# The recurrent block's gate of a decoder layer, multiplied in float32r parts

## The chip, the cores and the metric

The kernel runs on one core of a Trainium2 chip. The metric is the device time of one execution in microseconds (us), the median of several runs. TensorE is called PE in the profile (its weight loads PEld), VectorE DVE, ScalarE ACT, GpSimd POOL and SyncE SP.

## The reference

One decoder layer on 256 tokens with 2048 features in float32: a SwiGLU block, a mixer, cross attention into a memory, a second SwiGLU block and a last norm. The mixer is a sliding window attention beside an RWKV-7 time mixing. This is the part of the time mixing that the change touches:

```python
r, k, v, xw, xa, xg = jnp.split(xs, c, axis=-1)      # xg: 160 features
g = jax.nn.sigmoid(xg) @ g2.astype(f32)              # g2: (160, 1024)
...
y = rwkv7_scan(r, decay, k, v, -kk, kk * a)
mean = jnp.mean(y, axis=-1, keepdims=True)
var = jnp.mean(jnp.square(y - mean), axis=-1, keepdims=True)
y = ((y - mean) * lax.rsqrt(var + GN_EPS)).reshape(B, T, RWKV_WIDTH)
y = y * ln_w.astype(f32) + ln_b.astype(f32)
bonus = jnp.sum(r * k * r_k, axis=-1, keepdims=True) * v
y = (y + bonus.reshape(B, T, RWKV_WIDTH)) * g
```

The gate g is a product of 256 tokens x 160 features with 160 x 1024 weights. The result y is then multiplied by w_proj_rwkv.

## The kernel before

**Products in parts.** The large products don't run in float32. Each operand is split into two float32r parts: the high part is a cast on ACT (L345 for weights, L668 for activations), the low part is the rest, a subtraction on DVE (L346, L669). A product is then the sum of three float32r products, high x high, high x low and low x high (`times`, L438 to L440), accumulated in PSUM. Weights come in items of two blocks of 128 features by 512 columns; an item is used by 12 products (two blocks, two halves of the tokens, three parts). There are three buffers each for the high and the low parts (`hi`, `lo`), so the parts of an item are made up to two items ahead, and a cast can start when the item three before it has been used. A smaller float32 product, as those of the recurrent chain, takes its operands directly.

**Order of the work.** The large products run one after the other (`product`). After every six of TensorE's products there is a tick, at which each of several groups of background generators (`bg`: attn, ew, inverse, chain, norm and others) takes one step up to its next `yield`. Instructions are created in that order; a scheduler then orders each engine's queue by readiness, so that an engine's order can differ from the code's.

**The recurrent block.** It has two halves (h=0, 1) of 512 features each. `shifted` makes its inputs from the products with w_in (names r0, v0, r1, v1 are marked as seen when one is done); it uses a tile with the tag "d". `values(h)` turns v, `chain(h)` runs the recurrence and marks y0 or y1, and `finish(h)`, in the group norm, which runs one generator at a time, does the rest:

- it loads the half's columns of g2 (L1545, L1546) into a tile of two 128-row blocks, the last 32 of the 160 features in rows 96 to 127 of the second block, whose first 96 rows are set to zero (L1544);
- it takes the pair of tiles "sq" in `parted`, high and low (one buffer each, which `removal_keys` and `values` use too; the mark "parts" lets one user in at a time, `alone`), squares y into them (L1552, L1553, L1555), and sums the squares by head on TensorE (`head_sums`, L1154 with bdmean); ACT takes the root (L1557), DVE the reciprocal in four pieces with two ticks between (L1561) and the product with y (L1563);
- it multiplies the gate, float32, on TensorE (L1568): for each of four column blocks c of 128, two products of 128 rows with 256 token columns, the sigmoid of xg as the moving operand (`xg`, two blocks laid out as g2: the last 32 features in rows 96 to 127 of the second);
- DVE applies ln_w, the bonus, ln_b and the gate (L1574, L1577), and the result is split into `yr` (L668, L669), which the product with w_proj_rwkv reads.

While this runs, the foreground multiplies the four column blocks of the second gate by w_in (`gr`, L1598), and then uses yr.

Of the kernel before, what the change touches and what calls it, by code (L numbers as in the profile page):

```python
# [8 lines left out]
F32R = mybir.dt.float32r  # L9
AF = mybir.ActivationFunctionType  # L10
ALU = mybir.AluOpType
# [4 lines left out]
P = 128  # L16
T = 256
# [125 lines left out]
def decoder_layer(ctx: ExitStack, tc: tile.TileContext, a: dict, out: bass.AP):  # L143
    nc = tc.nc
    act, dve, pool, pe = nc.scalar, nc.vector, nc.gpsimd, nc.tensor
# [7 lines left out]
    bg = Interleave()  # L153
# [9 lines left out]
    def f32(x):  # L163
        return x.bitcast(F32)
# [4 lines left out]
    def two():  # L169
        return ps.tile([P, 2, 512], F32, tag="two", name="two", bufs=2)  # L170
# [18 lines left out]
    def wait_for(name):  # L189
        while name not in bg.seen:  # L190
            yield

    def idle(n):
        for _ in range(n):
            yield
# [96 lines left out]
    raws, parts = {}, {}  # L292
# [157 lines left out]
    def combinations(sp, x, seven, early, ready, tag, apart):  # L450
# [43 lines left out]
        return c  # L494

    def product_pair(x: Act, c, w, four, seven, early, after, end, finish, first=()):


# [33 lines left out]
        for q in range(late + 1):  # L532
# [22 lines left out]
            for i in range(KU):  # L555
                for to, t, j in (("p2", 0, 0), ("p4", 1, 0), ("p3", 0, 1), (p5, 1, 1)):
                    off = to == "p3" and q in early
                    ends = last and i == KU - 1
                    add(to, of_c(q, i) if off else of_x(t, k + i), u[i][j], ends)
                    if ends:  # L560
                        finish(to, b)
                    if t:
                        bg.tick()
# [3 lines left out]
    def gate_up(sp, x, c, r, w):  # L567
        hb = sp.tile([P, 2, 512], F32, tag="hb", name="hb", bufs=2)
        u2, u3 = (sp.tile([P, 512], F32, tag="u", name="u", bufs=2) for _ in range(2))

        def after(b):
            act.copy(hb[:, 0], b["p1"])

        def end(b):
            dve.tensor_tensor(u2[:], b["p6"], hb[:, 0], ALU.add)
            dve.tensor_tensor(u3[:], b["p7"], u2[:], ALU.add)
            dve.tensor_tensor(u2[:], b["p5"], u2[:], ALU.add)
            while c["next"]:
                bg.spawn("feat", c["next"].pop())

        def finish(to, b):
            if to == "p2":
                dve.tensor_tensor(hb[:, 0], b["p2"], hb[:, 0], ALU.add)
                act.activation(hb[:, 0], hb[:, 0], AF.Silu, scale=r[0])
            elif to == "p4":
                dve.tensor_tensor(hb[:, 1], b["p4"], u3[:], ALU.add)
                act.activation(hb[:, 1], hb[:, 1], AF.Silu, scale=r[1])
            else:
                t, v = (0, u2) if to == "p3" else (1, u3)
                dve.tensor_tensor(v[:], b[to], v[:], ALU.add)  # L590
                dve.scalar_tensor_tensor(
                    hb[:, t], v[:], r[t], hb[:, t], ALU.mult, ALU.mult
                )

        product_pair(x, c, w, False, SEVEN, EARLY, after, end, finish)
        return hb
# [69 lines left out]
    def split(x: Act, c, n, src):  # L666

        act.copy(x.at(0, c, n), src)  # L668
        dve.tensor_tensor(x.at(1, c, n), src, f32(x.at(0, c, n)), ALU.subtract)  # L669
        x.done |= set(range(c, c + n))  # L670
# [171 lines left out]
    with tc.tile_pool(name="f1", bufs=1, reuse_waits="tile") as sp:  # L842
        aligned(sp)
        at["pool"] = sp
        x = sp.tile([P, 2, D], F32, name="x")
# [46 lines left out]
    with tc.tile_pool(name="mx", bufs=1, reuse_waits="tile") as sp:  # L892
        aligned(sp)

        def t4(name, shape=(P, 4, T), dt=F32):
            return sp.tile(list(shape), dt, tag="t4", name=name, bufs=N4)
# [180 lines left out]
        xwa, xg = xs[:, 0, :], xs[:, 1:, :]  # L1077
# [66 lines left out]
        def parted(name):  # L1144
            return [
                sp.tile([P, 2, 512], F32R, tag=name + e, name=name + e, bufs=1)
                for e in ("hi", "lo")
            ]

        def head_sums(bd, parts):  # L1150
            b = two()
            for i in range(2):
                for j, part in enumerate(parts):
                    pe.matmul(b[:, i], bd[:], part[:, i], start=j == 0, stop=j == 1)  # L1154
            return b

        def alone():
            while "parts" in bg.seen:
                yield
            bg.seen.add("parts")  # L1160

        def wide4(x):
            return x[:].rearrange("p (a c) t -> p a (c t)", a=2)
# [103 lines left out]
        for n in range(4):  # L1267
            pg = product(n2.x, W["w_in"])
            g = t4("ga", (P, 2, 512))
# [54 lines left out]
        def room(name, shape):  # L1324
            return sp.tile(list(shape), F32, tag="mk", name=name, bufs=NMK)
# [81 lines left out]
        ek = dict(skip_group_check=True)  # L1407
# [127 lines left out]

        yr = Act([], [], 4)

        def finish(h):
            yield from wait_for(f"y{h}")
            for part in yr.parts:  # L1540
                part.append(t4("yr", dt=F32R))
            g2 = room("g2", (P, 2, 4 * P))
            f4 = slice(4 * h * P, (4 * h + 4) * P)
            pool.memset(g2[:96, 1, :], 0.0)  # L1544
            pool.dma_start(g2[:, 0, :], W["rwkv_g2"][:P, f4])  # L1545
            pool.dma_start(g2[96:, 1, :], W["rwkv_g2"][P:, f4])  # L1546
            y = yq[h]
            sq = room("sq", (P, 4, T))
            v = wide4(sq)
            yield from alone()  # L1550
            parts = parted("sq")
            act.activation(parts[0][:], wide4(y), AF.Square)  # L1552
            act.activation(sq[:], y[:], AF.Square)  # L1553
            yield
            dve.tensor_tensor(parts[1][:], v, f32(parts[0][:]), ALU.subtract)  # L1555
            yield from idle(2)
            act.activation(v, head_sums(bdmean, parts)[:], AF.Sqrt, bias=gneps[:])  # L1557
            bg.seen.discard("parts")
            yield
            for i in range(4):  # L1560
                dve.reciprocal(sq[:, i], sq[:, i])  # L1561
                yield from idle(2)
            dve.tensor_tensor(y[:], y[:], sq[:], ALU.mult)  # L1563
            yield
            b = two()[:].rearrange("p a (c t) -> p (a c) t", c=2)
            for c in range(4):
                for m in range(2):
                    pe.matmul(  # L1568
                        b[:, c], g2[:, m, c * P : (c + 1) * P], xg[:, m, :],
                        start=c % 2 + m == 0, stop=m == 1, **ek,  # L1570
                    )
            for c in range(4):
                f = slice(4 * h + c, 4 * h + c + 1)
                dve.scalar_tensor_tensor(  # L1574
                    y[:, c], y[:, c], ln_w[:, f], bv[h][:, c, :], ALU.mult, ALU.add
                )
                dve.scalar_tensor_tensor(y[:, c], y[:, c], ln_b[:, f], b[:, c], ALU.add, ALU.mult)  # L1577
                if c % 2:
                    split(yr, 4 * h + c - 1, 2, y[:, c - 1 : c + 1])
                    yield  # L1580
# [13 lines left out]
        for n in range(4):  # L1594
            pg = product(n2.x, W["w_in"])
            g = t4("gr", (P, 2, 512))
# [15 lines left out]
        for n in range(4):  # L1612
            m = t4("ml", (P, 2, 512))
            if n in kept:
                g = kept[n]
            else:
                g = t4("gl", (P, 2, 512))
# [79 lines left out]
        for mb in range(2):  # L1697
            for h in range(4):
                pe.matmul(
                    b4[h // 2][:, h % 2], vm[:, mb, h * P : (h + 1) * P], pt[mb][:, h, :],  # L1700
                    start=mb == 0 and h % 2 == 0, stop=mb == 1, skip_group_check=True,
# [13 lines left out]
    with tc.tile_pool(name="f2", bufs=1, reuse_waits="tile") as sp:  # L1715
        aligned(sp)
        at["pool"] = sp
        x = sp.tile([P, 2, D], F32, name="x")
# [110 lines left out]
```

## Time and profile before

| what | us |
|---|---|
| median of 3 runs (lowest 2220.95, highest 2223.41) | 2220.98 |
| the profiled execution | 2222.56 |
| its span, from the first to the last instruction | 2220.8 |
| DVE busy | 1759.2 |
| ACT busy | 1193.8 |
| the gate's records on TensorE (L1568), both halves | 7.2 |

The profile is of one execution. A line of a timeline gives the start in us from the span's start, the duration, the engine, the line of the code, the operation, the output and the inputs, the shapes and the number of records. A line of a group gives the busy time in all, the mean duration in ns, and the idle time of the engine before them with what ended it. Durations of TensorE's records overlap, since products are pipelined; the step from one start to the next tells what one costs. float32r operands of TensorE are shown as f32.

### The profile page before, as it was taken

What the parts mean: (1) busy time and instruction counts of PE and PEld (TensorE: products, weight loads), DVE (VectorE), ACT (ScalarE), POOL (GpSimd) and SP (SyncE); (2) the same over time, 40 slices, a digit from 0 to 9 for tenths busy, and PEclk for the clock granted to TensorE, in tenths of its full rate; (3) what the DMA queues carried; (4) which work ended last, traced back from release to release, by engine and by line L of the source; (5) the groups of instructions that cost most, each with busy time, mean ns of one, the idle gap of its engine ahead of it and who ended that gap; (6) DMA issues with size and microseconds to landing.
All of it is one profiled execution on the core that took longest, in us unless ns stands there. A gap on an engine that the chain in (4) does not pass through costs nothing.

```text
span 2220.8 us, 28313 instructions
## 1 busy us (share of the span) xinstructions
PE 2207.0 (99%) x10774; PEld 1817.7 (82%) x10774; DVE 1759.2 (79%) x2047; ACT 1193.8 (54%) x1438; POOL 72.0 (3%) x140
## 2 busy tenths in 40 slices
PE   9999999999999999999999999999999999999998
PEld 7788888888888877888888888888888888888886
DVE  8988988898887477878546576558888988898887
ACT  6555555555555557534434455456555555555554
POOL 1000000000000000010400000000000000000000
PEclk9999999999999999999999999999999999999999
DMA  7565665565556545677714665557565565565564
GB/s 266 200 219 193 204 208 190 190 209 192 206 183 217 169 131 159 210 226 224 203 55 146 229 219 202 187 168 259 199 204 184 200 209 190 189 208 193 205 207 154
DMA packets 220536, 433.31 MB, mean 195 GB/s; under 512 B 13952, under 2 KB 16336, under 8 KB 220400
## 3 DMA queue, kind: packets, MB, share of 16 engines
q1 hardware_dynamic: 213200, 410.70, 55.6%
q0 software_dynamic: 6624, 20.14, 2.9%
q8 instruction: 84, 1.38, 0.2%
q10 hardware_dynamic: 576, 0.66, 0.1%
q14 instruction: 52, 0.43, 0.1%
HBM read 419.00 MB, written 12.45 MB: 194 GB/s over the span
## 4 chain that ended last, share of the span: by engine, by line
PE 96%; DVE 1%; issue 1%; ACT 1%; DMA 0%; POOLq 0%; POOL 0%; SPq 0%; ACTq 0%; DVEq 0%
PE acc L438 21%; PE acc L439 20%; PE acc L440 20%; PE two L438 9%; PE two L439 9%; PE two L440 9%; PE two L187 2%; PE two L179 1%; DVE lo L346 1%; PE two L1351 0%; PE acc L1488 0%; PE acc L1453 0%; PE acc L1470 0%; PE two L1568 0%; PE acc L1351 0%
## 5 line engine op out<-in xcount | busy, mean ns | idle before, releaser
L345 ACT CAST hi<-raw 128x1024 fp32r<-128x1024 f32 (+1 forms) x769 | 764.0, 1003 | 794.3 <-PE two L440 370.6
L346 DVE TENSOR_TENSOR lo<-raw,hi 128x1024 fp32r<-128x1024 f32 (+1 forms) x770 | 884.2, 1158 | 325.0 <-ACT hi L345 323.7
L438 PE MATMUL acc<-hi,xhi 128*128 128x512 f32 (+1 forms) x1224 | 477.9, 391 | 1.1 <-ACT hi L345 0.7
L439 PE MATMUL acc<-lo,xhi 128*128 128x512 f32 (+1 forms) x1224 | 474.9, 388 | 0.9 <-DVE lo L346 0.9
L440 PE MATMUL acc<-hi,xlo 128*128 128x512 f32 (+1 forms) x1224 | 473.8, 387 | 0.0
L438 PEld LDWEIGHTS acc<-hi,xhi 128*128 128x128 f32 x1224 | 229.6, 188 | 53.3 <-issue 3.9
L439 PEld LDWEIGHTS acc<-lo,xhi 128*128 128x128 f32 x1224 | 229.8, 188 | 49.7 <-DVE lo L346 3.7
L440 PEld LDWEIGHTS acc<-hi,xlo 128*128 128x128 f32 x1224 | 229.8, 188 | 46.3 <-DVE xlo L712 0.2
L371 DVE TENSOR_TENSOR tlo<-raw,thi 128x1024 fp32r<-128x1024 f32 x160 | 193.1, 1220 | 0.0
L370 ACT CAST thi<-raw 128x1024 fp32r<-128x1024 f32 x160 | 165.8, 1051 | 33.4 <-DVE raw L365 19.1
L439 PE MATMUL acc<-lo,hhi 128*128 128x512 f32 x424 | 166.4, 392 | 0.0
L440 PE MATMUL acc<-hi,hlo 128*128 128x512 f32 x424 | 165.1, 389 | 0.0
L438 PE MATMUL acc<-hi,hhi 128*128 128x512 f32 x424 | 159.8, 391 | 0.1
L438 PE MATMUL two<-hi,xhi 128*128 128x512 f32 x352 | 138.4, 393 | 0.0
L439 PE MATMUL two<-lo,xhi 128*128 128x512 f32 x352 | 137.1, 390 | 0.0
L440 PE MATMUL two<-hi,xlo 128*128 128x512 f32 x352 | 137.0, 389 | 0.0
L365 DVE TENSOR_TENSOR raw<-raw 128x1024 f32<-128x1024 f32 x80 | 97.6, 1220 | 14.9 <-DMA raw<-in_ffn_w_up_dram 13.1
L439 PEld LDWEIGHTS acc<-lo,hhi 128*128 128x128 f32 x424 | 79.6, 188 | 19.3 <-DVE lo L346 3.1
L438 PEld LDWEIGHTS acc<-hi,hhi 128*128 128x128 f32 x424 | 79.1, 188 | 18.8 <-ACT hi L345 2.6
L440 PEld LDWEIGHTS acc<-hi,hlo 128*128 128x128 f32 x424 | 79.6, 188 | 16.3
L438 PEld LDWEIGHTS two<-hi,xhi 128*128 128x128 f32 x352 | 66.1, 188 | 15.0 <-DVE u L590 0.5
L440 PEld LDWEIGHTS two<-hi,xlo 128*128 128x128 f32 x352 | 66.1, 188 | 13.9
(392 smaller groups left out, 3190.2 us busy)
## 6 DMA issues: line engine op xcount, KB each, us to landing
raw<-in_ffn_w_gate_dram SPq DMA_DIRECT2D x171, 512.0 KB, 3.7
raw<-in_ffn_w_up_dram SPq DMA_DIRECT2D x167, 512.0 KB, 4.6
raw<-in_ffn_w_down_dram SPq DMA_DIRECT2D x152, 512.0 KB, 4.7
raw<-in_w_in_dram SPq DMA_DIRECT2D x136, 512.0 KB, 3.5
raw<-in_w_out_dram SPq DMA_DIRECT2D x32, 512.0 KB, 3.6
raw<-in_ffn_w_down_dram SPq DMA_DIRECT2D x12, 1024.0 KB, 5.1
raw<-in_w_proj_attn_dram SPq DMA_DIRECT2D x16, 512.0 KB, 3.6
raw<-in_w_proj_rwkv_dram SPq DMA_DIRECT2D x16, 512.0 KB, 4.2
```

The lines of the kernel that those rows point to most:

```text
L179: prev = pe.matmul(to, lhs, rhs, **how)
L187: prev = pe.transpose(to, src, ident[:])
L345: newest["act"] = act.copy(hi[:, s], raw[:, s])
L346: newest["dve"] = dve.tensor_tensor(lo[:, s], raw[:, s], f32(hi[:, s]), ALU.subtract)
L365: dve.tensor_tensor(ta[:], raw[:, 1:3], raw[:, 0:2], ALU.subtract)
L370: act.copy(hi[:, s], t[:])
L371: dve.tensor_tensor(lo[:, s], t[:], f32(hi[:, s]), ALU.subtract)
L438: pe.matmul(o, xh, hi, start=first, stop=False, **how)
L439: pe.matmul(o, xh, lo, start=False, stop=False, **how)
L440: newest["pe"] = pe.matmul(o, xl, hi, start=False, stop=last, **how)
```

## The change

The gate is multiplied in float32r parts. Once, at h=0 and behind a wait for v1, the moving operand is split into a tile `xp` with the tag "d": block 0 is the high part of the first 128 features, block 1 their low part, and block 2 holds the last 32 features in four groups of 32 rows: zero, high, low, high. For each half g2's first 128 features are split into the high and the low tile of the pair "sq" (block 0), and block 1 of the high tile holds its last 32 features in groups zero, low, high, high. A column block c is then the sum of four float32r products with 256 token columns: high x high, high x low, low x high, and one of the stacked groups, in which low x high, high x low and high x high of the last 32 features lie beside each other. The mark "parts" is kept until the gate has been multiplied. The memset of g2's 96 rows goes.

```diff
         def finish(h):
             yield from wait_for(f"y{h}")
             for part in yr.parts:
                 part.append(t4("yr", dt=F32R))
+            yield from wait_for("v1")
+            if h == 0:
+                gate.append(sp.tile([P, 4, T], F32R, tag="d", name="xgp"))
+                xp, tail = gate[0], xg[96:, 1]
+                pool.memset(f32(xp[:32, 2]), 0.0)
+                act.copy(xp[:, 0], xg[:, 0])
+                for q in (96, 32):
+                    act.copy(xp[q : q + 32, 2], tail)
+                dve.tensor_tensor(xp[:, 1], xg[:, 0], f32(xp[:, 0]), ALU.subtract)
+                dve.tensor_tensor(xp[64:96, 2], tail, f32(xp[96:, 2]), ALU.subtract)
+                yield
+            xp = gate[0]
             g2 = room("g2", (P, 2, 4 * P))
             f4 = slice(4 * h * P, (4 * h + 4) * P)
-            pool.memset(g2[:96, 1, :], 0.0)
             pool.dma_start(g2[:, 0, :], W["rwkv_g2"][:P, f4])
             pool.dma_start(g2[96:, 1, :], W["rwkv_g2"][P:, f4])
...
             act.activation(v, head_sums(bdmean, parts)[:], AF.Sqrt, bias=gneps[:])
-            bg.seen.discard("parts")
-            yield
+            yield
+            gh, gl = parted("sq")
+            gt, tail = gh[:, 1], g2[96:, 1]
+            pool.memset(f32(gt[:32]), 0.0)
             for i in range(4):
                 dve.reciprocal(sq[:, i], sq[:, i])
+                if i == 0:
+                    act.copy(gh[:, 0], g2[:, 0])
+                elif i == 1:
+                    for q in (96, 64):
+                        act.copy(gt[q : q + 32], tail)
+                elif i == 2:
+                    dve.tensor_tensor(gl[:, 0], g2[:, 0], f32(gh[:, 0]), ALU.subtract)
+                    dve.tensor_tensor(gt[32:64], tail, f32(gt[96:]), ALU.subtract)
                 yield from idle(2)
             dve.tensor_tensor(y[:], y[:], sq[:], ALU.mult)
             yield
             b = two()[:].rearrange("p a (c t) -> p (a c) t", c=2)
             for c in range(4):
-                for m in range(2):
+                for m, (g, x) in enumerate(
+                    ((gh[:, 0], 0), (gh[:, 0], 1), (gl[:, 0], 0), (gt, 2))
+                ):
                     pe.matmul(
-                        b[:, c], g2[:, m, c * P : (c + 1) * P], xg[:, m, :],
-                        start=c % 2 + m == 0, stop=m == 1, **ek,
+                        b[:, c], g[:, c * P : (c + 1) * P], xp[:, x, :],
+                        start=c % 2 + m == 0, stop=m == 3, **ek,
                     )
+            bg.seen.discard("parts")
```

More of the change, by code (lines that the diff above doesn't have):

```diff
@@ L1536, in decoder_layer @@
         yr = Act([], [], 4)
+        gate = []
         def finish(h):
```

## The prediction

> **What bounds the kernel now.** I read the page first (busy shares, granted clock, chain), then the list of waits of TensorE alone, then the timelines of the stage in which the gate is multiplied.
>
> ```profile
> span 2220.8 us, 28313 instructions
> PE 2207.0 (99%) x10774; PEld 1817.7 (82%) x10774; DVE 1759.2 (79%) x2047; ACT 1193.8 (54%) x1438; POOL 72.0 (3%) x140
> PEclk9999999999999999999999999999999999999999
> PE 96%; DVE 1%; issue 1%; ACT 1%; DMA 0%; POOLq 0%; POOL 0%; SPq 0%; ACTq 0%; DVEq 0%
> ```
>
> TensorE (PE) is busy 99% of the span at the full clock, and 96% of the chain that ended last is TensorE. A busy share could still hide a bad stage, so the next view is what TensorE waited for over the whole span:
>
> ```profile
> PE acc L204 <- POOL ones L199: 1.1, 1, 1.1
> PE two L187 <- ACT tok L907: 1.0, 2, 0.6
> PE acc L439 <- DVE lo L346: 0.9, 2, 0.6
> PE acc L438 <- ACT hi L345: 0.7, 2, 0.5
> ```
>
> These are its four longest waits, none above 1.1 us. So the time is the sum of what the products take, and a product that streams faster shortens the kernel by just that, as long as TensorE is still fed. Now the gate itself, its two blocks (h=0, then h=1):
>
> ```profile
> 1200.75 3.62 PE L1568 MATMUL two<-xs,g 128*128 128x256 f32 x16
> 1204.02 0.58 PE L438 MATMUL acc<-hi,xhi 128*128 128x512 f32 x1
> 1204.44 0.39 PE L439 MATMUL acc<-lo,xhi 128*128 128x512 f32 x1
> ...
> 1226.95 3.62 PE L1568 MATMUL two<-xs,g 128*128 128x256 f32 x16
> 1230.22 0.58 PE L438 MATMUL acc<-hi,xhi 128*128 128x512 f32 x1
> 1230.64 0.39 PE L439 MATMUL acc<-lo,xhi 128*128 128x512 f32 x1
> ```
>
> Starts are the first column. Each block has 8 products in the code but 16 records: a float32 product runs as two. Durations of records overlap, so I use starts. In the float32r stream the step from start to start is:
>
> ```profile
> 1204.89 0.39 PE L438 MATMUL acc<-hi,xhi 128*128 128x512 f32 x1
> ...
> 1212.15 0.39 PE L440 MATMUL acc<-hi,xlo 128*128 128x512 f32 x1
> ```
>
> These are the first and the last of 33 records: 7.26 us / 32 = **0.2269 us** for 512 columns. After a gate block the first L438 takes 0.42 us to the next start (1204.02 to 1204.44), the rest of the switch from float32. So a block costs, from its start to that second start less one ordinary step, 1204.44 - 1200.75 - 0.227 = **3.463 us**, and the same for h=1 (1230.64 - 1226.95 - 0.227). Both: 6.93 us.
>
> **The change part by part.**
>
> *The products.* Per block 8 float32 products go, and 16 float32r products with 256 columns come. No float32r product of 256 columns is in this trace. The nearest are those of the 288 column weights:
>
> ```profile
> L438 PE MATMUL acc<-hi,xhi 128*128 128x288 f32 x32 | 10.2, 319 | 0.0
> ...
> L1568 PE MATMUL two<-xs,g 128*128 128x256 f32 x32 | 7.2, 379 | 0.0
> ```
> ```profile
> 810.98 0.29 PE L438 MATMUL acc<-hi,xhi 128*128 128x288 f32 x1
> ...
> 812.84 0.29 PE L440 MATMUL acc<-hi,xlo 128*128 128x288 f32 x1
> ```
>
> The product with 288 columns has 16 feature blocks and two token halves, so 32 products per part and 32 records: one record each, where the gate's 16 float32 products gave 32. The second fence holds the first and the last of 15 records: 1.86 us / 14 = 0.1329 us. Between 512 and 288 columns a column costs (0.2269 - 0.1329) / 224 = 0.00042 us, so 256 columns cost 0.1329 - 32 x 0.00042 = **0.1195 us**. The block: 16 x 0.1195 = 1.91 us, and no switch of type at its end. Gain per block 3.463 - 1.91 = 1.55 us, for both **3.10 us**.
>
> Bounds. Upwards, a narrower product isn't dearer than one of 512 columns: 16 x 0.2269 = 3.63 us, a loss of 0.17 per block, +0.3 in all. Downwards, half of the 512-column step, 0.1135, gives 1.82 per block and a gain of 3.3 in all. Do the weight loads allow that step? Every product loads its own 128x128 weights, and the shortest streams show what loads alone allow:
>
> ```profile
> 1168.15 1.89 PE L1470 MATMUL acc<-u,xb 128*128 128x64 f32 x16
> ```
> ```profile
> L438 PEld LDWEIGHTS acc<-hi,xhi 128*128 128x128 f32 x1224 | 229.6, 188 | 53.3 <-issue 3.9
> ```
>
> 16 records of only 64 columns take 1.89 us, 0.118 us each: that is the pace of loading, just at my 0.1195. I take 0.1195, from the nearest row.
>
> Of the skill, one rule speaks against this gain and one states a smaller step. The Trainium skill, "TensorE: Matmul & The Clock Gate", Part 3, "The mechanism", says that a weight load overlaps running matmuls only when it goes to another group of rows. By that rule each of these products, which all use all rows, would cost its load and its stream one after the other, the price of rival B; the 0.1329 us step, shorter than the 0.188 us load record alone, disagrees. The same page's "Back-to-back issue gap" gives N/2.4 + 2.5 ns, as an estimate 109 ns for 256 columns, by which the gain would be 3.4 us; the trace's 288 columns took 133 ns where that formula gives 122.
>
> *The parts.* They are new work on ACT and DVE. Rows of like length (32 partitions cost as much as 128):
>
> ```profile
> L668 ACT CAST yr<-yq 128x512 fp32r<-128x512 f32 x4 | 2.5, 622 | 6.8 <-DVE yq L1577 6.8
> ...
> L1366 ACT COPY n<-acc 32x512 f32<-32x512 f32 x4 | 2.3, 578 | 3.3 <-PE acc L1351 3.2
> ...
> L1018 ACT CAST yahi<-acc 128x256 fp32r<-128x256 f32 x4 | 1.6, 389 | 0.3 <-PE acc L179 0.3
> L1377 ACT COPY xb<-acc 32x256 f32<-32x256 f32 x4 | 1.5, 365 | 4.6 <-issue 3.0 <-PE acc L1351 1.1 <-DVE xu L1379 0.5
> ...
> L669 DVE TENSOR_TENSOR yr<-yq,yr 128x512 fp32r<-128x512 f32 x4 | 2.7, 686 | 0.1
> ...
> L1019 DVE TENSOR_TENSOR yalo<-acc,yahi 128x256 fp32r<-128x256 f32 x4 | 1.7, 420 | 0.0
> ```
>
> Per block, ACT gets 0.62 + 2 x 0.58 = 1.78 us and DVE 2 x 0.69 = 1.37. Once, for the moving operand, ACT gets 0.39 + 2 x 0.365 = 1.12 and DVE 2 x 0.42 = 0.84. Together ACT 4.68, DVE 3.58, in all 8.26 us beside TensorE. I cost them at nothing; what hides them is the lead of the weight parts, tightest here:
>
> ```profile
> 1214.00:1228.00 14.00, 14.00 (x63) 11.63 (x62) 12.80 (x10) 9.59 (x10) 1.80 (x3) 1.00 0.66 203
> ```
> ```profile
> 1221.62 3.35 DVE L1561 RECIPROCAL sq<-sq 128x256 f32<-128x256 f32 x2
> 1224.88 2.29 DVE L346 TENSOR_TENSOR lo<-raw,hi 128x1024 fp32r<-128x1024 f32 x2
> ```
>
> In this stretch (columns: PE, PEld, DVE, ACT busy) DVE is at 12.80 of 14 us, and 1.37 more overfills it. Its two weight parts of 1224.88 end at 1226.04 and 1227.17. The first is used behind the gate block, which would now end at 1226.95 + 1.91 = 1228.9 instead of 1230.4; delayed by 1.37 it is there at 1227.4, 1.5 us early. The second is there at 1228.5 and used one item (12 products, 2.72 us) later. The gate's own low parts, made between the two reciprocals, are there at about 1223.3 + 1.37 = 1224.7, for 1226.95. If this cover were gone, the 8.26 us would count in full.
>
> *The held buffer.* The parts of g2 use the pair of tiles that held the squares, and keep it until the gate's products are done. Today the squares of h=1 go into it before the products of h=0:
>
> ```profile
> 1193.18 1.06 ACT L1552 ACTIVATE sqhi<-yq 128x1024 fp32r<-128x1024 f32 x1
> ...
> 1198.94 1.22 DVE L1555 TENSOR_TENSOR sqlo<-sq,sqhi 128x1024 fp32r<-128x1024 f32 x1
> ```
> ```profile
> 1212.38 0.40 PE L1154 MATMUL two<-sqhi,bdmean 128*128 128x512 f32 x1
> ```
>
> They will have to wait for the products' end, about 1200.75 + 1.91 + 0.26 = 1202.9 (0.26 is the last record's 0.379 less its step). Then 1.07 on ACT and 1.22 on DVE: ready at 1205.2, if nothing else stands ahead. Their sums L1154 come due at 1212.38 - 1.55 = 1210.8. There are 5.6 us to spare; queued behind L1552 are weight casts with the lead above. Cost: nothing; bound, if two casts and two DVE groups of 1.2 us go ahead, still inside the 5.6.
>
> *The waits and the POOL queue.* `finish` now waits for v1, before its first instruction:
>
> ```profile
> 1129.08 1.67 DVE L1061 SCALAR_TENSOR_TENSOR bv<-d,v_rwkv,p 128x256 f32<-128x256 f32 x4
> ```
> ```profile
> 1149.56 1.04 PE L1301 MATMUL two<-ident,bv 128*128 128x128 f32 x8
> ```
> ```profile
> 1153.60 1.06 ACT L1553 ACTIVATE sq<-yq 128x1024 f32<-128x1024 f32 x1
> ```
>
> DVE ends v1's shift at 1130.75 and TensorE turns v1 at 1149.56, while the first work of `finish` on ACT starts at 1153.60: it costs nothing. On POOL, each block's memset of 96x512 is exchanged for one of 32x512, and one of 32x256 comes once; behind them in POOL's queue are g2's DMAs and the stores of the other gate, and POOL is busy 3%. No DMA is added. And the result is not in a hurry:
>
> ```profile
> 1235.89 0.69 DVE L669 TENSOR_TENSOR yr<-yq,yr 128x512 fp32r<-128x512 f32 x1
> ```
> ```profile
> 1268.50 0.39 PE L438 MATMUL acc<-hi,yr 128*128 128x512 f32 x1
> ```
>
> The last part of yr ends 32 us before its first use.
>
> *The sum.* Products -3.10, all else 0: the profiled execution would go from 2222.56 us (span 2220.8 and 1.76 around it) to 2219.5. It lies 1.58 above the median of the three runs, 2220.98; from that median the forecast is **2217.9 us**.
>
> **The rivals.**
>
> A. *The 256 columns don't stream in one pass.* No float32r row here is narrower than 288. If 256 lay below a limit, each of 32 products would cost two records, as float32 does: 3.463 / 8 = 0.433 us, 13.86 in all, 6.93 more than now: 2227.9, slower. It decides at 0.2165 us per product, where 32 of them equal today's 6.93. Against it: 288 is only 32 columns away and one record each.
>
> B. *The weight load isn't hidden.* Then a product costs 0.188 + 0.1195 = 0.3075 us, 4.92 per block, +2.9: 2223.9. Against it stands the 0.1329 us step. It is what the Trainium skill's rule on row groups, cited above, would make of this kernel.
>
> C. *The narrow products go at the pace of 512 columns*: +0.3, 2221.3. Against it again the 288 columns.
>
> D. *TensorE starves.* The queues' order isn't written by hand: ACT runs L1552 of h=1 at 1193.18, before the yr casts of h=0, against the code's order:
>
> ```profile
> 1205.31 0.62 ACT L668 CAST yr<-yq 128x512 fp32r<-128x512 f32 x1 [3.32 <-DVE yq L1577]
> ```
>
>  If the new copies go ahead of weight casts around 1215 to 1230, TensorE waits in L438 or L439. It costs up to 8.26: 2217.9 to 2226.1, in the middle 2222. The sign turns at 3.1 us of waiting.
>
> E. *More is gained*, from queues that fall better and runs that scatter: the waits listed above add up to 3.7 us in the whole span, so at most some 2216.
>
> **How the numbers follow.** A measurement of this kernel tells about 0.2%, 4.4 us, from no change: 2216.5 to 2225.4. Chances: forecast 0.64, A 0.05, B 0.04, C 0.05, D 0.17, E 0.05. Faster by more: E and 0.05 of the forecast by scatter (the runs shown span 2.5 us), 0.10. Slower by more: A, about half of D, and a little of B by scatter, 0.15. Within: 0.75. The range runs from 2216.5, the forecast with the 3.3 us bound and scatter, to 2224.5, over C, B and the lower part of D; it leaves out A, the upper half of D and the end of E.
>
> **What would show it.** Right: the gate's 32 products in 32 records with a step near 0.12 us, blocks of about 1.9 us, no 0.42 us step behind them, and TensorE's waits as short as now. The squares of h=1 on ACT at about 1203 and L1154 without a wait. Wrong: two records per product (A), a step near 0.31 (B) or 0.23 (C), or waits of TensorE for L345, L346, the squares or the new parts that add up to more than 3 us (D).

## The result, and the profile after

| | us |
|---|---|
| before, median of 21 runs | 2221.65 (2220.61 to 2225.25) |
| changed, median of 21 runs | 2218.52 (2217.45 to 2219.86) |
| ratio | 0.9985, 95% interval 0.9979 to 0.9991 |
| difference of the medians | -3.13 |
| changed, profiled execution | 2218.37, span 2216.6 |

The kernel became faster by 0.15%, clear of noise, and inside the band of 0.2%. The forecast was -3.10 us; its 2217.9 started from a median of three runs, 2220.98, where 21 runs give 2221.65. That the medians agree with it to 0.03 us is finer than their interval, which runs from -4.7 to -2.0 us, and so is luck. The top of the changed kernel's page, and what its TensorE waited for in all:

```profile
span 2216.6 us, 28327 instructions
PE 2202.8 (99%) x10774; PEld 1816.7 (82%) x10774; DVE 1761.8 (79%) x2053; ACT 1197.5 (54%) x1447; POOL 72.2 (3%) x141
PEclk9999999999999999999999999999999999999999
PE 96%; DVE 1%; DMA 1%; ACT 1%; issue 1%; SPq 0%; POOLq 0%; POOL 0%; ACTq 0%; DVEq 0%
```
```profile
PE acc L439 <- DVE lo L346: 1.3, 4, 0.6
PE acc L204 <- POOL ones L199: 1.1, 1, 1.1
PE acc L438 <- ACT hi L345: 0.8, 2, 0.6
PE two L187 <- DVE s L980: 0.6, 1, 0.6
```

Nothing changed in kind: the same share, the same clock, waits as short as before (5.1 us in all before, 5.0 after, by the full lists). TensorE ran as many records, 10774: 32 of the gate before, 32 now, since a float32 product was two records and there are now twice as many products of one each. The two gate blocks of the changed kernel, in the timeline of TensorE:

```profile
1199.29 0.40 PE L1593 MATMUL two<-xgp,sqhi 128*128 128x256 f32 x2
...
1201.08 0.28 PE L1593 MATMUL two<-xgp,sqhi 128*128 128x256 f32 x1
1201.20 0.39 PE L438 MATMUL acc<-hi,xhi 128*128 128x512 f32 x1
1201.43 0.40 PE L439 MATMUL acc<-lo,xhi 128*128 128x512 f32 x1
...
1223.95 0.40 PE L1593 MATMUL two<-xgp,sqhi 128*128 128x256 f32 x2
...
1225.74 0.28 PE L1593 MATMUL two<-xgp,sqhi 128*128 128x256 f32 x1
1225.86 0.39 PE L438 MATMUL acc<-hi,xhi 128*128 128x512 f32 x1
1226.09 0.40 PE L439 MATMUL acc<-lo,xhi 128*128 128x512 f32 x1
```

Counted as before (start of the block to the second start behind it, less one step of 0.227), a block is 1201.43 - 1199.29 - 0.227 = 1.91 us, and the second the same. The step is (1201.20 - 1199.29) / 16 = 0.119 us. The L438 behind the block is 0.23 us from the next start, not 0.42: the slow step behind the block is gone.

**Where the difference sits.** Two single profiles also scatter outside the changed part: at the first start of the recurrent chain's last line (L1518) the changed kernel was already 1.4 us ahead (1127.4 against 1128.8 in the rows below), before the first cast into `xp`, at 1129.3. So I measure the stage: from the last start of L1518 to the first product that reads yr, within one execution. Before, then changed; in each row the numbers behind the colon are the least, median and greatest duration in ns, then the first and the last start:

```profile
L1518 PE MATMUL acc<-sa,bk x16: 275/275/275, 1128.8 to 1178.3; 128*128 128x128 f32 x16
```
```profile
L438 PE MATMUL acc<-hi,yr x64: 389/389/478, 1268.5 to 1314.0; 128*128 128x512 f32 x64
```
```profile
L1518 PE MATMUL acc<-sa,bk x16: 275/276/276, 1127.4 to 1176.8; 128*128 128x128 f32 x16
```
```profile
L438 PE MATMUL acc<-hi,yr x64: 388/390/479, 1264.0 to 1309.5; 128*128 128x512 f32 x64
```

1268.5 - 1178.3 = 90.2 us before, 1264.0 - 1176.8 = 87.2 us after: -3.0 us, the two blocks' 2 x 1.55. The same two rows give this for each kernel of the study:

| kernel | stage, us | against before | a gate block, us |
|---|---|---|---|
| before | 90.2 | | 3.46 |
| changed | 87.2 | -3.0 | 1.91 |
| changed, again | 87.2 | -3.0 | 1.91 |
| e1, parts only | 90.2 | 0.0 | 3.46 |
| e8, first half only | 88.7 | -1.5 | 1.91 and 3.46 |
| e3, 128 columns | 90.5 | +0.3 | 3.6 |
| e5, 32 rows | 92.2 | +2.0 | 4.4 |
| e9, 32 rows last | 89.9 | -0.3 | 3.24 |
| e4, parts twice | 87.3 | -2.9 | 1.91 |
| e4, parts four times | 92.3 | +2.1 | 1.91; the second torn apart |

### The profile page after: what moved, and what is told of

Its sections match the earlier page's. It is cut to its first block, busy times and chain, and to the rows that moved or that the text cites. A ratio compares the mean times of both kernels' runs of the same rounds, so it can differ in the third digit from the quotient of the medians.

```text
span 2216.6 us, 28327 instructions
## 1 busy us (share of the span) xinstructions
PE 2202.8 (99%) x10774; PEld 1816.7 (82%) x10774; DVE 1761.8 (79%) x2053; ACT 1197.5 (54%) x1447; POOL 72.2 (3%) x141
## 4 chain that ended last, share of the span: by engine, by line
PE 96%; DVE 1%; DMA 1%; ACT 1%; issue 1%; SPq 0%; POOLq 0%; POOL 0%; ACTq 0%; DVEq 0%
PE acc L438 21%; PE acc L439 21%; PE acc L440 21%; PE two L438 9%; PE two L439 9%; PE two L440 9%; PE two L187 2%; PE two L179 1%; DMA raw<-in_ffn_w_up_dram 1%; DVE lo L346 1%; PE two L1351 0%; PE acc L1488 0%; PE acc L1453 0%; PE acc L1470 0%; PE acc L1351 0%
## 5 line engine op out<-in xcount | busy, mean ns | idle before, releaser
L345 ACT CAST hi<-raw 128x1024 fp32r<-128x1024 f32 (+1 forms) x769 | 762.8, 1001 | 791.8 <-PE two L440 370.5
L346 DVE TENSOR_TENSOR lo<-raw,hi 128x1024 fp32r<-128x1024 f32 (+1 forms) x770 | 884.3, 1158 | 321.2 <-ACT hi L345 320.0
L438 PE MATMUL acc<-hi,xhi 128*128 128x512 f32 (+1 forms) x1224 | 478.1, 391 | 1.2 <-ACT hi L345 0.8
L438 PEld LDWEIGHTS acc<-hi,xhi 128*128 128x128 f32 x1224 | 229.7, 188 | 52.9 <-issue 3.9
L438 PE MATMUL acc<-hi,hhi 128*128 128x512 f32 x424 | 160.0, 391 | 0.1
L438 PE MATMUL two<-hi,xhi 128*128 128x512 f32 x352 | 138.5, 393 | 0.0
L438 PEld LDWEIGHTS acc<-hi,hhi 128*128 128x128 f32 x424 | 79.2, 188 | 18.8 <-ACT hi L345 2.6
L438 PEld LDWEIGHTS two<-hi,xhi 128*128 128x128 f32 x352 | 66.1, 188 | 14.7 <-DVE u L590 0.2
```

The source lines that it names most:

```text
L345: newest["act"] = act.copy(hi[:, s], raw[:, s])
L346: newest["dve"] = dve.tensor_tensor(lo[:, s], raw[:, s], f32(hi[:, s]), ALU.subtract)
L438: pe.matmul(o, xh, hi, start=first, stop=False, **how)
```

## The experiments

Theory: the whole gain is that TensorE streams the gate faster, and everything else of the change is hidden. Rivals: moved work gains something too; the parts cost something that the products pay for. Beside them stands the question of what bounds such a narrow product, and what the stack of four groups is worth. e1, e8, e3 and e5 ran on one chip with 33 runs of before (median 2222.26), the other four on another (median 2221.88).

**e1: all of the change but its products.**

```diff
+            pool.memset(g2[:96, 1, :], 0.0)
             pool.dma_start(g2[:, 0, :], W["rwkv_g2"][:P, f4])
...
-                for m, (g, x) in enumerate(
-                    ((gh[:, 0], 0), (gh[:, 0], 1), (gl[:, 0], 0), (gt, 2))
-                ):
+                for m in range(2):
                     pe.matmul(
-                        b[:, c], g[:, c * P : (c + 1) * P], xp[:, x, :],
-                        start=c % 2 + m == 0, stop=m == 3, **ek,
+                        b[:, c], g2[:, m, c * P : (c + 1) * P], xg[:, m, :],
+                        start=c % 2 + m == 0, stop=m == 1, **ek,
                     )
```

> All of the change but its products: the new wait, the parts of both operands, the held buffer and the later release of the mark stay; the gate's products are the float32 ones of before, with g2's zeros back. Theory (the whole gain is TensorE's streaming, all else is hidden): the time of before, ratio 1.000 within 0.0005, blocks of 3.46 us, TensorE's waits no longer than in before. Rival (part of the gain comes from moved work): faster than before by 0.5 us or more. Rival (the parts aren't hidden and the change pays for them): slower than before by 0.5 us or more.

Measured: 2222.65 us, ratio 1.0003 (0.9994 to 1.0012). The interval is too wide for a rival of 0.5 us, but the stage takes 90.2 us, to the tenth that of before. The parts, the wait for v1 and the late mark cost and gain nothing that shows. Two things are not tested here, as no float32 product reads the tiles with the parts: whether the parts are there in time, and the held buffer (ACT writes the squares of h=1 into it at 1192.93, as early as in before, 1193.18). For both, see the changed kernel's own trace, further down. What is left as the source of the gain is the products.

**e8: only the first half.** `finish(1)` keeps the float32 products, and makes no parts of g2.

```diff
+                if h:
+                    for m in range(2):
+                        pe.matmul(
+                            b[:, c], g2[:, m, c * P : (c + 1) * P], xg[:, m, :],
+                            start=c % 2 + m == 0, stop=m == 1, **ek,
+                        )
+                    continue
                 for m, (g, x) in enumerate(
```

> Only the first half's gate (h=0) is multiplied in parts; the second half is multiplied in float32 as before. Theory (each block gives 1.55 us by itself): 1.55 us faster than before, 2220.1; first block 1.91 us, second 3.46. Rival (what is gained depends on the tight stretch behind the second block, or comes in one lump): much more or much less than half of the 3.1 us.

Measured: 2220.23 us, ratio 0.9992 (0.9982 to 1.0001), stage -1.5 us. The medians alone hardly tell it from before; by the stage and the blocks (1.91 and 3.46 us), each block gives its half.

**e10: the changed kernel again**, unedited, beside the last three.

> The changed kernel once more, beside the next three on one chip. Theory: 3.1 us faster than before (ratio 0.9986), blocks of 1.91 us.

Measured: 2218.75 us, ratio 0.9985 (0.9976 to 0.9994), stage 87.2.

**e3: products of 128 columns.**

```diff
-                    pe.matmul(
-                        b[:, c], g[:, c * P : (c + 1) * P], xp[:, x, :],
-                        start=c % 2 + m == 0, stop=m == 3, **ek,
-                    )
+                    for t in range(2):
+                        ts = slice(t * P, (t + 1) * P)
+                        pe.matmul(
+                            b[:, c, ts], g[:, c * P : (c + 1) * P], xp[:, x, ts],
+                            start=c % 2 + m + t == 0, stop=m == 3, **ek,
+                        )
```

> Each of the changed kernel's gate products is cut into two of 128 token columns, 32 a block. It tells what bounds a narrow float32r product. If weight loading sets the pace at 0.118 us (as in the 64-column float32 stream), a block takes 32 x 0.118 = 3.8 us and the kernel is 3.7 us slower than the changed one, as slow as before or a little slower (2221.5 to 2222.5). If streaming alone sets it (0.1195 less 128 x 0.00042 = 0.066 us), a block takes 2.1 us and the kernel is 0.4 us slower than the changed one (2218.9). Theory: the load, since 0.118 is the shortest step of any 128x128 weights in the trace.

Measured: 2222.31 us, ratio 1.0 (0.9991 to 1.0009). Its first block in the timeline:

```profile
1199.57 0.56 PE L1595 MATMUL two<-xgp,sqhi 128*128 128x128 f32 x4
...
1202.87 0.39 PE L1595 MATMUL two<-xgp,sqhi 128*128 128x128 f32 x2
```

30 products lie between these starts: 3.30 / 30 = 0.110 us each. Half the columns save only 0.009 us of 0.119. So something other than streaming bounds, as expected, at 0.110. The 0.118 of the expectation was misread: it is a duration, 1.89 us, divided by 16. By starts the float32 stream of 64 columns agrees with e3, 1169.88 - 1168.15 = 1.73 us for 16 records, 0.108 each. That it is the load, and not a fixed cost of each product, is supported, not proven, by another stream in the trace of before, with weights of only 64 columns. The first line is the product behind the 64-column stream:

```profile
1169.88 0.61 PE L1499 MATMUL two<-ident,kk 128*128 128x128 f32 x4
...
1174.58 1.09 PE L1488 MATMUL acc<-mk,vtok 128*64 128x128 f32 x16
1175.50 1.04 PE L1488 MATMUL acc<-mk,sa 128*64 128x128 f32 x16
```

Here 16 records with 128 streamed columns take 0.92 us, 0.058 each: half the weights, about half the step. (These products go by turns to two halves of the output rows; what that alone is worth is not shown.) The gate's 256 columns lie 0.009 us above e3's pace: nothing is left to gain by narrower products.

**e5: no stack.** The last 32 features run as three products of 32 rows, all in rows 96 to 127 (high x high, high x low, low x high). The copies into other groups and the zeros go.

```diff
-                for m, (g, x) in enumerate(
-                    ((gh[:, 0], 0), (gh[:, 0], 1), (gl[:, 0], 0), (gt, 2))
-                ):
+                for m, (g, x) in enumerate((
+                    (gh[:, 0], xp[:, 0]), (gh[:, 0], xp[:, 1]), (gl[:, 0], xp[:, 0]),
+                    (gh[96:, 1], xp[96:, 2]), (gh[96:, 1], xp[96:, 3]),
+                    (gl[96:, 1], xp[96:, 2]),
+                )):
```

> The last 32 features aren't stacked: each column block takes three products of 32 rows (96 to 127) in place of the one of four groups, 24 products a block instead of 16. If a product of 32 rows costs what one of 128 costs (0.1195 us), a block takes 2.87 us, 0.96 more, and the kernel is 1.9 us slower than the changed one (2220.4). If 32 rows are cheaper, or overlap, less than that; if TensorE empties at each change between 128 and 32 rows (8 changes a block), more, and visible as longer steps at the changes. Theory: 1.9 us slower.

Measured: 2226.2 us, ratio 1.0018 (1.0009 to 1.0027). The theory falls: instead of 1.9 us it is 5.0 us slower than the changed kernel by the stage (92.2 against 87.2), and some 7 by the medians (3.9 above before, which is itself 3.1 above the changed kernel). The start of its first block:

```profile
1199.89 0.28 PE L1591 MATMUL two<-xgp,sqlo 128*128 128x256 f32 x1
1200.10 0.50 PE L1591 MATMUL two<-xgp,sqhi 32*128 32x256 f32 x2
1200.44 0.28 PE L1591 MATMUL two<-xgp,sqlo 32*128 32x256 f32 x1
1200.65 0.50 PE L1591 MATMUL two<-xgp,sqhi 128*128 128x256 f32 x2
```

The shape before the operands (128*128, 32*128) says how many rows are in use. From the last product of 128 rows to the first of 32 there are 0.21 us instead of 0.12, and the two records behind it take 0.34 to the third start instead of 0.24. Each change costs some 0.19 us, and eight of them are the 1.53 us that a block of 4.40 has over 24 x 0.1195. The blocks make 2 x 2.49 = 5.0 us against the changed kernel, which is also what the stage shows. The rest of the median goes with the granted clock: four of its ten runs have 0.999 and take 2224.3 to 2225.3 us, near what the stage says (2222.26 + 2.0); six have 0.998 and take 2226.0 to 2228.5. None of these six was profiled, so why the clock is lower there stays open; the last run of this section shows what such a drop can look like.

**e9: the products of 32 rows last.** Two changes a block instead of eight, the same 24 products.

```diff
+            whole = (gh[:, 0], xp[:, 0]), (gh[:, 0], xp[:, 1]), (gl[:, 0], xp[:, 0])
+            rest = (
+                (gh[96:, 1], xp[96:, 2]), (gh[96:, 1], xp[96:, 3]), (gl[96:, 1], xp[96:, 2])
+            )
+            for pairs in (whole, rest):
+                for c in range(4):
+                    for m, (g, x) in enumerate(pairs):
```

> The kernel with three products of 32 rows per column block again, but all twelve of 128 rows come first in a block and all twelve of 32 rows after them, so that TensorE changes the number of rows once on the way in and once on the way out instead of eight times. In the run with eight changes a block took 4.40 us, 1.53 more than 24 x 0.1195. Theory (the 1.53 is eight changes at 0.19 us each): 2.87 + 2 x 0.19 = 3.25 us a block, the kernel 2.7 us slower than the changed one. Rival (32 rows are dearer by themselves, 0.11 to 0.13 us each): a block stays near 4.4 us.

Measured: 2222.29 us, ratio 1.0 (0.9991 to 1.001).

```profile
1199.24 0.40 PE L1592 MATMUL two<-xgp,sqhi 128*128 128x256 f32 x2
...
1202.37 0.50 PE L438 MATMUL acc<-hi,xhi 128*128 128x512 f32 x1
1202.71 0.40 PE L439 MATMUL acc<-lo,xhi 128*128 128x512 f32 x1
```

A block is 1202.71 - 1199.24 - 0.227 = 3.24 us, expected 3.25, and the stage is 2.7 us longer than the changed kernel's, as expected (the medians on this chip lie 3.5 apart, with intervals of 2 us to either side). So 32 rows cost what 128 cost, and it is the change of rows that costs.

**e4: the parts made twice, and four times.** Every copy and subtraction of the parts is repeated in place.

```diff
                 if i == 0:
-                    act.copy(gh[:, 0], g2[:, 0])
+                    for _ in range(4):
+                        act.copy(gh[:, 0], g2[:, 0])
```

> Each copy and each subtraction that makes the parts runs twice, so that ACT gets 4.7 us and DVE 3.6 us more than in the changed kernel. Theory (their cost is hidden by the lead of the weight parts, and DVE has some 1.3 us to spare behind the second block): within 0.4 us of the changed kernel, TensorE's waits at most 0.5 us longer in all. Rival (the change pays for its parts): slower by as much as the change itself pays, up to 8.3 us.

Measured: 2219.73 us, ratio 0.9989 (0.998 to 0.9998); the stage takes 87.3 us, 0.1 more than in the changed kernel. The median is 1.0 above the changed kernel's on the same chip, where at most 0.4 was expected, but the intervals don't separate the two. TensorE's waits add up to 5.7 us, against 5.2 in e10: 0.5 longer, as much as was expected at most. The gate's low parts of h=1 end at 1224.43 and their block starts at 1225.34: 0.9 us are left, less than one more round of 1.37 us on DVE.

> The same work four times, so ACT gets 14.0 us and DVE 10.7 us more than in the changed kernel, 5.3 and 4.1 of them in the tight stretch around the second block. Theory (the lead there is about 1.3 to 2.5 us): now it shows, TensorE waits for the gate's low parts or for weight parts by 2 to 4 us, 2220.5 to 2222.5. Rival (the lead is much larger): still within 0.4 us of the changed kernel. Rival (nothing of it is hidden): 25 us slower.

Measured: 2224.74 us, ratio 1.0012 (1.0003 to 1.0021). All ten runs lie above the expected 2220.5 to 2222.5: it is slower than the theory said. The stage takes 92.3 us, 5.1 more than the changed kernel's. What TensorE waited for between 1100 and 1260 us:

```profile
PE acc L439 <- DVE lo L346: 1.5, 2, 0.8
PE acc L438 <- ACT hi L345: 1.2, 1, 1.2
```

The changed kernel has no wait for either line in that stretch. So the cover exists and ends between two and four times the work. Of the 5.1 us 2.7 stand as waits of these lines, inside the expected 2 to 4. The second block is torn apart: its first two products start at 1224.64, the third, the first to read the low parts, at 1229.69, with products of the weights between them. And these run slowly:

```profile
1226.70 0.63 PE L439 MATMUL acc<-lo,xhi 128*128 128x512 f32 x1
...
1229.69 0.41 PE L1597 MATMUL two<-xgp,sqlo 128*128 128x256 f32 x1
```

Seven products of 512 columns lie between these starts, 2.99 us / 7 = 0.427 us each instead of 0.227. The granted clock from 1226.40 to 1230.00 is 0.53; in the same window of before it is 1.00. These seven alone cost 1.4 us more, and about 1.0 us of the 5.1 isn't told apart. It comes right behind TensorE's stalls for these two lines (1.2 and 0.8 us, the longest ones above); that they bring the clock down is not shown by a run of its own. The expectation counted the waits alone.

## Why the prediction was right

**The products**, the one term of the sum. 0.1195 us a product was read between the 512 and the 288 columns; measured 0.119, block 1.91 as forecast. It held because the line through two widths stays straight down to 256, which the prediction assumed, and because the floor that e3 shows, 0.110, lies below it. The prediction's own check of that floor was misread: 0.118 was a duration divided by 16, against its own rule to go by starts, by which the same row gives 0.108. So the margin was 0.011 us and not 0.0015: the reading erred on the safe side, and the forecast didn't use it.

**The switch of type** is 0.19 us of each block's 1.55; the other 1.36 is 16 records at 0.204 us (3.27 / 16) that became 16 at 0.119. The 0.19 is measured; that the type is its cause is only argued. Behind e3's blocks, which have the type of the stream, the first L438 also takes 0.28 us (1203.09 to 1203.37) instead of 0.227.

**The parts at nothing**: confirmed by e1 for the work on ACT and DVE, and by the changed kernel's trace for their coming in time. Durations came out as read: in the changed kernel a cast of 128x512 takes 0.61 us, two copies of 32x512 1.25 (forecast 1.16), the subtractions 0.63 and 0.69. The stretch of the second block, on DVE:

```profile
1218.61 1.74 DVE L1576 RECIPROCAL sq<-sq 128x256 f32<-128x256 f32 x1
1220.27 0.63 DVE L1583 TENSOR_TENSOR sqlo<-g,sqhi 128x512 fp32r<-128x512 f32 x1
1220.93 0.69 DVE L1584 TENSOR_TENSOR sqhi<-g,sqhi 32x512 fp32r<-32x512 f32 x1
1221.65 1.23 DVE L346 TENSOR_TENSOR lo<-raw,hi 128x1024 fp32r<-128x1024 f32 x1
1222.79 1.75 DVE L1576 RECIPROCAL sq<-sq 128x256 f32<-128x256 f32 x1
1224.45 1.16 DVE L346 TENSOR_TENSOR lo<-raw,hi 128x1024 fp32r<-128x1024 f32 x1
```

The gate's low parts end at 1221.62, 2.3 us before the block at 1223.95; forecast 2.2. The spare time of the weight part behind the block was sized too small: I put it behind the fourth reciprocal, 1.5 us early, but the scheduler put it ahead (1221.65). It ends at 1222.88 for a use at 1226.09, 3.2 us early. This fits with e4, where twice the work is still hidden.

**The held buffer**: the squares of h=1 did have to move, and it cost nothing. On ACT, and then the sums on TensorE:

```profile
1201.46 1.06 ACT L1565 ACTIVATE sqhi<-yq 128x1024 fp32r<-128x1024 f32 x1 [0.92 <-PE two L1593]
```
```profile
1209.37 0.40 PE L1154 MATMUL two<-sqhi,bdmean 128*128 128x512 f32 x1
```

The bracket is the predicted wait: ACT stood idle for 0.92 us until the gate's products released the tile. The low part of the squares followed on DVE from 1203.88 to 1205.10, behind one group of yr's, and the sums came 4.3 us later without a wait; forecast were 5.6 us to spare with nothing ahead.

**The rivals.** A fell with one record per product. B fell with the step: load and stream one after the other would be 0.3 us, and e3's 0.110 is shorter than a load record (0.192 there). The rule on row groups of the Trainium skill's "TensorE: Matmul & The Clock Gate", Part 3, "The mechanism", as the prediction cites it, does not hold for these products, which all use the same rows; the section itself also names a background weight buffer as a target that lets a load run ahead. The estimate of 0.109 us a product and a gain of 3.4 us fell as well, with 0.119 and 3.1. C fell with the step too. D did not happen, but e4 shows it as a real mechanism with the predicted signs (L345 and L346), at four times the work. E did not happen (its bound was also wrong: 2217.9 less waits of 3.7 us is 2214.2, not 2216): the span of one profile was 4.2 us shorter, but the stage shows 3.0, and the rest is scatter between executions.

## What to carry to other kernels

Where TensorE is busy all the time and waits for nothing, price a change by starts of its records, not by durations: count records, read the step for the nearest widths, and look at the step behind the block for a switch. Small remainders of a contraction are best stacked into rows that stand empty: here one product of four groups of rows instead of three of 32 rows saved 5 us, of which 3 were changes of the number of rows; against the better order of e9 it saves 2.7. And work that goes to other engines is free only as far as the parts they feed have a lead; repeating that work in place shows how far that is.

## What the runs showed of the hardware that was not expected

- A change between products of 128 and of 32 rows costs some 0.19 us (e5: eight changes 1.53 us; e9: two changes 0.37 us, 3.24 less 24 x 0.1195). The Trainium skill, "TensorEngine Tiling (Array Packing)", "Key Properties", says that a change of tiling mode drains TensorE; these runs fit that, and give the price.
- With every product loading its own 128x128 float32r weights, the step at 512, 288, 256 and 128 columns is 0.227, 0.133, 0.119 and 0.110 us: down to 256 the columns count, below that a floor of 0.110 does. Float32 records with weights of 128x64 go every 0.058 us (L1488 in before, by turns to two halves of the output rows), which speaks against a fixed cost per product; the load of the weights is what fits.
- In one execution (e4, four times the work), right behind stalls of 1.2 and 0.8 us, the granted clock was 0.53 from 1226.40 to 1230.00, and products of 512 columns took 0.427 us instead of 0.227. Seven of them cost 1.4 us beside the stalls; that the stalls brought the clock down is not shown.
